# Score matmuls ahead of the key copy, a smaller warm-up tile, a second queue for the last store, and no transfers from GpSimd

## The chip, the cores and the metric

One Trainium2 chip, one of its cores. Five engines work side by side, each through its own list of instructions in order: TensorE (PE, with its weight loads shown as PEld), VectorE (DVE), ScalarE (ACT), GpSimd (POOL) and SyncE (SP), which here only issues transfers. They wait for each other through semaphores. The metric is device microseconds of one execution of the whole program, and times of a kernel are given as the median over its runs.

## The reference

One decoder layer on 1024 prompt tokens and 8 x 8 sample tokens, model width 1024. All is float32. What matters of it:

```python
proj = jnp.einsum('btd,de->bte', x, w_in)
u, gp, q, k, v, gg, fa = jnp.split(proj, SPLIT_IDX, axis=-1)
pool_out, new_buf = pool_mix(u, buf, start_pos, w_map, pool_scale)      # windows 2, 4, 8, 16
log_a = jax.nn.log_sigmoid(fa @ w_a2 + b_a) / GLA_TAU
o, S_new = gla_chunked(q * 64 ** -0.5, k, v, log_a, S)                  # 4 heads, running state S
o = o * lax.rsqrt(jnp.mean(o * o, axis=-1, keepdims=True) + RMS_EPS) * norm_g
mix = jnp.concatenate([pool_out * silu(gp), o * silu(gg)], axis=-1)
h = DEEPNORM_ALPHA * x + mix @ w_out
out = (h - mean(h)) * lax.rsqrt(var(h) + LN_EPS) * ln_g + ln_b
```

The outputs are the layer's `out` for both kinds of tokens, the new pooling buffers and the new states S.

## The kernel before, in words

Tokens lie in nine tiles: eight of 128 prompt tokens (0 to 7) and one of 64 sample tokens (8). For the projections they are grouped in three column chunks of 384, 384 and 320. To keep float32 accuracy each operand is split into a high part (`hi`, rounded to the matmul's format, a ScalarE copy, line 61) and a low part (`lo`, the rest, a VectorE subtraction, line 64), and `mm3` (lines 66 to 70) makes three matmuls of each product: hi x hi, hi x lo, lo x hi. `mm2` does the same for the sample tile.

The order of work is written out by hand; no scheduler moves anything in the part that runs (`manual_schedule`). The stages are:

- **Head.** Input pieces are loaded by SP (the very first by ScalarE), split, and multiplied into the value projection `psv` in eight k-slices. Ahead of that, nine idle matmuls run on a cleared tile `warm` into `psw` (line 189). GpSimd clears `warm` and some other tiles first.
- **Projection groups.** `group(i, c)` computes 128 output columns `i` for the tokens of column chunk `c`, 24 matmuls into `psm`. The order is k, q, u (the pooling input), gp and gg (the gates). At `c == 0` the next weights are split and the ones after that loaded: `load_w` puts a load of 512 KB on SP's queue, into one of two `raw` buffers, so it waits until the buffer's last content was split.
- **Linear attention, interleaved.** `later(delay, fn)` and `tick()` put short pieces between the projection groups; a piece runs at the first tick whose number has reached its due time, and pieces of one tick run in the order of their due times. For chunk c (one token tile) the pieces are `s1a` (turn the keys with two transposes into the bank `pskt`, and copy them to `kt`), `s1b` (four score matmuls per chunk and the mask), `s2p` (keys x values into `psp_`, the state's growth), `s2` (state and masked scores applied, squares, and the state's decay) and `s3` (norm). At one tick they come as: `s1a` of chunk c+1, `s2p` of chunk c, `s1b` of chunk c+1, `s2` of chunk c. The sample tile, chunk 8, has its own times (AT8).
- **Output.** Nine output tiles: `mix @ w_out` into `pso`, then residual, mean and variance, and two VectorE passes with `lng` (the layer norm's gain and bias, broadcast over the partitions). A store `o_y` per tile goes out on SP. The last tile (TAIL) is worked in halves and stored in two pieces, both on SP.

All small PSUM tiles (`pskt`, `psa1`, `psp_`, `pso1`, `psms`, `psmap`) come from one pool of six banks in rotation; `psm` and `psv` have a pool of two. The bank `pskt` holds two things: the turned keys in its first 256 columns and, behind them, the scores of heads 0 and 2 (`pa[0] = pk[:, 256:]`). An access of a bank by one engine waits for the access of another engine to the same bank, whatever the columns. So the scores wait for ScalarE's copy of the turned keys.

GpSimd issues four transfers in the part that runs: `o_sp` (the prompt's final state, line 789, 128 KB), `o_npool` (the pooling buffers, line 485, 270 KB), and the two loads of `lng` (lines 490 and 491, 512 KB each).

The file also holds a second body (`safe`), for inputs whose decay is too strong; it runs only when a flag computed on the way says so, and doesn't run here.

Of the kernel before, what the change touches and what calls it, by code (L numbers as in the profile page):

```python
# [7 lines left out]
F32 = mybir.dt.float32  # L8
FR = mybir.dt.float32r
# [30 lines left out]
class Body:  # L40
# [54 lines left out]
    def emit(self):  # L95
# [82 lines left out]
        rst = ep.tile([128, 384], F32, name="rst")  # L178
        rst2 = ep.tile([128, 320], F32, name="rst2")
        nc.gpsimd.memset(wa2r, 0.0)  # L180
        nc.gpsimd.memset(sel, 0.0)
        nc.gpsimd.memset(eps[:, 0:1], RMS_EPS)
        nc.gpsimd.memset(eps[:, 1:2], LN_EPS)
        nc.scalar.preload_act_table_set(EXP_LN)
        warm = et.tile([128, 512], F32, tag="ab", name="warm")
        nc.gpsimd.memset(warm, 0.0)
        psw = psg.tile([128, 512], F32, tag="g", name="psw")
        for _ in range(9):
            nc.tensor.matmul(psw, warm[:, :128].bitcast(FR), warm.bitcast(FR), start=True, stop=True)  # L189

# [291 lines left out]
        for i in range(4, 16):  # L482
            if i == 14:
                assert not self.due
                nc.gpsimd.dma_start(io["o_npool"], npool)
                for name in ["gl", "pt", "kq"]:
                    self.close(name)
                lnp = self.pool("ln", 1)
                lng = lnp.tile([128, 2, D], F32, name="lng")
                nc.gpsimd.dma_start(lng[:, 0], io["ln_g"].partition_broadcast(128))  # L490
                nc.gpsimd.dma_start(lng[:, 1], io["ln_b"].partition_broadcast(128))
                load_res(0)
                load_res(1)
            for c in range(3):
                group(i, c)
            if i == 14:
                for k in (3, 4, 5):
                    load_wo(k)
# [5 lines left out]
        def out_tile(t):  # L504
# [40 lines left out]
            for cs in parts:  # L545
                nc.vector.scalar_tensor_tensor(hh[:n, cs], hh[:n, cs], mv[:n, 3:4], lng[:n, 1, cs],
                                               op0=ALU.mult, op1=ALU.add)
                nc.sync.dma_start(io["o_y"][t * 128:t * 128 + n, cs], hh[:n, cs])

# [132 lines left out]
    def gla_steps(self, c):  # L682
# [29 lines left out]
        def s1a():  # L712
# [8 lines left out]
            pk = g_tile("pskt")  # L721
            pa = [pk[:, 256:], None]
            for p in range(2):
                nc.tensor.transpose(pk[:n, p * 128:(p + 1) * 128], Kst[:, p], self.ident)
            kt = self.kt8 if sample else gl.tile([128, 256], F32, tag="kt", bufs=1 if self.safe else 2, name="kt")
            nc.scalar.activation(kt[:n], pk[:n, :256], AF.Copy)
            st["kt"], st["pa"] = kt, pa

        def s1b():
            am, pa, Qi = st["am"], st["pa"], st["Qi"]  # L730
            if not self.safe:
                pa[1] = g_tile("psa1")
                for h in range(4):
                    r, p = rows[h % 2], h // 2
                    nc.tensor.matmul(pa[h % 2][:n, p * n:(p + 1) * n], K[r, p], Q[r, p], start=True, stop=True)  # L735
                for e in range(2):
                    nc.vector.tensor_tensor(am[:n, two(e), :n], pa[e][:n, :2 * n].rearrange("s (p t) -> s p t", p=2),
                                            msk[:n, :n].unsqueeze(1).broadcast_to([n, 2, n]), op=ALU.mult)
# [33 lines left out]
        def decay():  # L772
# [15 lines left out]
            if c == 7:  # L788
                nc.gpsimd.dma_start(self.io["o_sp"], sn)

# [70 lines left out]
    def safe_scores(self, c, am, t0, n, sample):  # L861
# [17 lines left out]
        while True:  # L879
# [19 lines left out]
            ml = gl.tile([128, 128], F32, tag="lv", bufs=1, name="lv")  # L899
            nc.gpsimd.dma_start(ml, self.io["lvs" if sample else "lvp"][:, lev])  # L900
            mb = ml[:n, :n].unsqueeze(1).broadcast_to([n, 2, n])
# [23 lines left out]
TAIL = 7  # L925
# [108 lines left out]
```

## Time and profile before

| | us |
|---|---|
| runs shown, median of 3 (lowest, highest) | 398.11 (397.14, 398.34) |
| the profiled execution | 397.98 |
| its span, first to last instruction | 396.2 |
| TensorE busy | 383.3 (97%) |
| VectorE busy | 217.7 (55%) |
| ScalarE busy | 143.6 (36%) |
| GpSimd busy | 8.6 (2%) |
| transfers, mean over the span | 87 GB/s |

The rows shown below come from one profiled execution. A row of the timeline has the start and the duration in microseconds, the engine, the line of the kernel, the operation, the tile written and the tiles read, and in brackets how long the engine had been idle before it and what ended that. A row of the waits has the engine and tile that waited, the work that released it, the sum in microseconds, how many times, and the longest. A row of one line's instructions has the least, the median and the greatest duration in nanoseconds. Queues of issued transfers are named SPq and ACTq.

### The profile page before, as it was taken

How to read it: one execution, taken by the hardware profiler on the slowest of the kernel's cores; microseconds unless marked ns; L12 is line 12 of the kernel's file. 1: busy time of each engine (PE TensorE's matmuls, PEld its weight loads, DVE VectorE, ACT ScalarE, POOL GpSimd, SP SyncE). 2: the span in 40 equal slices, each digit the busy share in tenths (PEclk: the TensorE clock that was granted, in tenths of full speed). 3: DMA queues.
4: the chain of work that ended last, by engine and by line, in shares of the span. 5: the costliest groups of instructions: out<-in, count | busy, mean ns of one | idle time of the engine just before them, and what ended most of it. 6: DMA issues, size and time to landing. Idle time of an engine off the chain costs nothing.

```text
span 396.2 us, 6088 instructions
## 1 busy us (share of the span) xinstructions
PE 383.3 (97%) x2473; PEld 358.3 (90%) x2473; DVE 217.7 (55%) x429; ACT 143.6 (36%) x273; POOL 8.6 (2%) x31
## 2 busy tenths in 40 slices
PE   8999999999999999999999999999999999999991
PEld 7999999999989999999899899999988888888790
DVE  4775555621354778788433321333399565556683
ACT  5554554410023425435766222421283333211200
POOL 1000000000000000000001000100000000000000
PEclk9999999999999999999999999999999999999996
DMA  7960001011100101030103110443330253242321
GB/s 257 393 237 2 19 36 55 3 51 53 55 19 36 53 2 52 3 141 20 55 0 97 53 37 17 161 160 101 132 141 10 96 213 106 108 159 79 103 84 60
DMA packets 11556, 34.29 MB, mean 87 GB/s; under 512 B 1776, under 2 KB 3232, under 8 KB 11264
## 3 DMA queue, kind: packets, MB, share of 16 engines
q1 hardware_dynamic: 10960, 32.24, 23.7%
q0 software_dynamic: 416, 1.46, 1.1%
q8 instruction: 21, 0.34, 0.3%
q10 hardware_dynamic: 144, 0.14, 0.1%
q14 instruction: 15, 0.12, 0.1%
HBM read 27.91 MB, written 5.91 MB: 85 GB/s over the span
## 4 chain that ended last, share of the span: by engine, by line
PE 93%; ACT 3%; issue 1%; DVE 1%; POOL 0%; ACTq 0%; POOLq 0%
PE psm L68 15%; PE psm L69 15%; PE psm L70 15%; PE pso L68 7%; PE pso L69 7%; PE pso L70 7%; PE psv L69 4%; PE psv L68 4%; PE psv L70 4%; PE pskt L735 1%; PE psw L189 1%; PE pso L75 1%; PE pso L78 1%; PE pso L804 1%; PE psms L833 1%
## 5 line engine op out<-in xcount | busy, mean ns | idle before, releaser
L68 PE MATMUL psm<-xc,hl 128*128 128x384 f32 (+1 forms) x384 | 126.2, 329 | 0.0
L70 PE MATMUL psm<-xc,hl 128*128 128x384 f32 (+1 forms) x384 | 125.4, 327 | 0.0
L69 PE MATMUL psm<-xc,hl 128*128 128x384 f32 (+1 forms) x384 | 125.3, 326 | 0.0
L68 PEld LDWEIGHTS psm<-xc,hl 128*128 128x128 f32 x384 | 72.1, 188 | 0.7 <-issue 0.2
L69 PEld LDWEIGHTS psm<-xc,hl 128*128 128x128 f32 x384 | 72.2, 188 | 0.1
L70 PEld LDWEIGHTS psm<-xc,hl 128*128 128x128 f32 x384 | 72.1, 188 | 0.0
L68 PE MATMUL psv<-wv,xc 128*128 128x264 f32 x128 | 36.9, 288 | 0.0
L70 PE MATMUL psv<-wv,xc 128*128 128x264 f32 x128 | 36.7, 287 | 0.0
L69 PE MATMUL psv<-wv,xc 128*128 128x264 f32 x128 | 36.7, 286 | 0.0
L68 PE MATMUL pso<-wo,mx 128*128 128x512 f32 (+1 forms) x85 | 32.0, 377 | 0.0
L70 PE MATMUL pso<-wo,mx 128*128 128x512 f32 (+1 forms) x85 | 32.0, 377 | 0.0
L69 PE MATMUL pso<-wo,mx 128*128 128x512 f32 (+1 forms) x85 | 32.0, 377 | 0.0
L539 ACT ACTIVATE mv<-mv,eps 128x1 f32<-128x1 f32 (+1 forms) x9 | 2.7, 295 | 64.8 <-DVE mv L538 64.8
L403 DVE SCALAR_TENSOR_TENSOR vm<-sg,vecs,vm 128x128 f32<-128x128 f32 (+1 forms) x36 | 10.3, 340 | 27.8 <-ACT sg L397 27.8
L64 DVE TENSOR_TENSOR hl<-raw,hl 128x1024 fp32r<-128x1024 f32 x19 | 23.2, 1223 | 3.8 <-ACT hl L61 3.5
L644 ACT ACTIVATE ue<-psm 128x384 f32<-128x384 f32 (+1 forms) x12 | 5.5, 456 | 53.4 <-PE psm L70 49.5
L68 PEld LDWEIGHTS psv<-wv,xc 128*128 128x128 f32 x128 | 24.6, 192 | 0.1
L69 PEld LDWEIGHTS psv<-wv,xc 128*128 128x128 f32 x128 | 24.5, 191 | 0.1
L532 DVE SCALAR_TENSOR_TENSOR hh<-xr,pso 128x512 f32<-128x512 f32 (+2 forms) x19 | 12.4, 654 | 21.8 <-PE pso L70 21.6
L70 PEld LDWEIGHTS psv<-wv,xc 128*128 128x128 f32 x128 | 24.4, 190 | 0.0
L61 ACT ACTIVATE hl<-raw 128x1024 fp32r<-128x1024 f32 x19 | 19.9, 1051 | 6.4 <-PE psm L70 6.4
L68 PE MATMUL pso<-hl,mx 128*128 128x512 f32 (+1 forms) x51 | 19.3, 379 | 0.0
(236 smaller groups left out, 587.3 us busy)
## 6 DMA issues: line engine op xcount, KB each, us to landing
raw<-wm_dram SPq DMA_DIRECT2D x16, 512.0 KB, 3.5
xr<-x_dram SPq DMA_DIRECT2D x8, 512.0 KB, 4.3
o_y_dram<-hh SPq DMA_DIRECT2D x7, 512.0 KB, 2.9
wr<-w_out_dram SPq DMA_DIRECT2D x5, 512.0 KB, 4.5
s<-s_dram SPq DMA_DIRECT2D x2, 1024.0 KB, 6.7
hl<-xt_dram SPq DMA_DIRECT2D x2, 768.0 KB, 7.0
raw<-w_out_dram SPq DMA_DIRECT2D x3, 512.0 KB, 3.4
hl<-xt_dram SPq DMA_DIRECT2D x2, 640.0 KB, 5.4
```

The lines of the kernel that those rows point to most:

```text
L61: self.nc.scalar.activation(hi.bitcast(FR), raw, AF.Copy)
L64: (on_lo or self.nc.vector).tensor_tensor(lo.bitcast(FR), raw, hi, op=ALU.subtract)
L68: nc.tensor.matmul(ps, ahi.bitcast(FR), bhi.bitcast(FR), start=first, stop=False)
L69: nc.tensor.matmul(ps, ahi.bitcast(FR), blo.bitcast(FR), start=False, stop=False)
L70: nc.tensor.matmul(ps, alo.bitcast(FR), bhi.bitcast(FR), start=False, stop=last)
L75: one = lambda st, sp: nc.tensor.matmul(ps, both.bitcast(FR), bhi.bitcast(FR), start=st, stop=sp)
L78: nc.tensor.matmul(ps[:64], both[:, :64].bitcast(FR), blo.bitcast(FR), start=False, stop=False)
L189: nc.tensor.matmul(psw, warm[:, :128].bitcast(FR), warm.bitcast(FR), start=True, stop=True)
L403: nc.vector.scalar_tensor_tensor(pg, sg[:, to:to + tn], self.norm[:, m:m + 1], pg, op0=ALU.mult, op1=ALU.mult)
L532: nc.vector.scalar_tensor_tensor(hh[:n, s], x[:n, s], ALPHA if n == 128 else 1.0, ps[h][:n, :wd], op0=ALU.mult, op1=ALU.add)
L644: nc.scalar.activation(ue[:, HIST:HIST + np_], src[:, :np_], AF.Copy)
L735: nc.tensor.matmul(pa[h % 2][:n, p * n:(p + 1) * n], K[r, p], Q[r, p], start=True, stop=True)
```

## The change

It has four parts.

1. In `s1a` only the two transposes stay. The copy to `kt` becomes a function `keys()`, called in `s1b` after the four score matmuls and before the masks (in the `safe` body it stays where it was). The bank is the same.
2. `warm` is 128 x 128 in place of 128 x 512, and is cleared first of all on GpSimd; the idle matmuls read it four times over by a broadcast and are as wide as before.
3. The last tile's first half is stored by ScalarE's queue, the second by SP's as before.
4. The four transfers of GpSimd (and the ones of the `safe` body) are issued by SP.

```diff
+        warm = et.tile([128, 128], F32, tag="ab", name="warm")
+        nc.gpsimd.memset(warm, 0.0)
         nc.gpsimd.memset(wa2r, 0.0)
...
-        warm = et.tile([128, 512], F32, tag="ab", name="warm")
-        nc.gpsimd.memset(warm, 0.0)
         psw = psg.tile([128, 512], F32, tag="g", name="psw")
+        wide = warm.bitcast(FR).unsqueeze(1).broadcast_to([128, 4, 128])
         for _ in range(9):
-            nc.tensor.matmul(psw, warm[:, :128].bitcast(FR), warm.bitcast(FR), start=True, stop=True)
+            nc.tensor.matmul(psw.rearrange("p (a c) -> p a c", a=4), warm.bitcast(FR), wide, start=True, stop=True)
...
-                nc.gpsimd.dma_start(io["o_npool"], npool)
+                nc.sync.dma_start(io["o_npool"], npool)
...
-                nc.gpsimd.dma_start(lng[:, 0], io["ln_g"].partition_broadcast(128))
-                nc.gpsimd.dma_start(lng[:, 1], io["ln_b"].partition_broadcast(128))
+                nc.sync.dma_start(lng[:, 0], io["ln_g"].partition_broadcast(128))
+                nc.sync.dma_start(lng[:, 1], io["ln_b"].partition_broadcast(128))
...
-                nc.sync.dma_start(io["o_y"][t * 128:t * 128 + n, cs], hh[:n, cs])
+
+                q = nc.scalar if t == TAIL and cs.start == 0 else nc.sync
+                q.dma_start(io["o_y"][t * 128:t * 128 + n, cs], hh[:n, cs])
...
-            pa = [pk[:, 256:], None]
+            pa = [pk[:, 256:], None, pk]
             for p in range(2):
                 nc.tensor.transpose(pk[:n, p * 128:(p + 1) * 128], Kst[:, p], self.ident)
+            st["pa"] = pa
+            if self.safe:
+                keys()
+
+        def keys():
             kt = self.kt8 if sample else gl.tile([128, 256], F32, tag="kt", bufs=1 if self.safe else 2, name="kt")
-            nc.scalar.activation(kt[:n], pk[:n, :256], AF.Copy)
-            st["kt"], st["pa"] = kt, pa
+            nc.scalar.activation(kt[:n], st["pa"][2][:n, :256], AF.Copy)
+            st["kt"] = kt
...
                     nc.tensor.matmul(pa[h % 2][:n, p * n:(p + 1) * n], K[r, p], Q[r, p], start=True, stop=True)
+
+                keys()
                 for e in range(2):
...
-                nc.gpsimd.dma_start(self.io["o_sp"], sn)
+                nc.sync.dma_start(self.io["o_sp"], sn)
```

On TensorE no instruction moves; what changes is which of them wait. This is its list at the turn from chunk 1 to chunk 2, before (`pskt` and `psa` get the scores, `psp_` the keys x values; the numbers behind names are buffers, and a wait names the engine whose semaphore is waited for):

```order
L724 MATMUL pskt<-ident,K 128x128 [waits PE_49]
L766 MATMUL psp__1462<-vm,kt 64x128 [waits Activation_49]
L735 MATMUL pskt<-Q,K 128x128 [waits Activation_49]
L735 MATMUL psa_1468<-Q,K 128x128
L802 MATMUL psp__1462<-Q,S 128x128
L802 MATMUL pso_1475<-Q,S 128x128
```

And the same place in the changed kernel (its lines 727, 776, 743 and 812):

```order
L727 MATMUL pskt<-ident,K 128x128 [waits PE_49]
L776 MATMUL psp__1460<-vm,kt 64x128 [waits Activation_49]
L743 MATMUL pskt<-Q,K 128x128
L743 MATMUL psa_1466<-Q,K 128x128 [waits Activation_49]
L812 MATMUL psp__1460<-Q,S 128x128
L812 MATMUL pso_1475<-Q,S 128x128 [waits Activation_49]
```

The first score matmul has no wait left. Two waits for ScalarE stand there now that the one for the copy had covered: `psa` takes a bank that ScalarE's `rs` (line 838 before) read last, and `pso` one that `pmix` (line 675 before) read last, both in the group before. On ScalarE the copy keeps its place in the list, but now waits for the scores in place of the transposes, and on VectorE the mask of `pskt` waits for that copy.

SP's list, from the flag's reading to the first loads of the output stage, before:

```order
L200 DMA raw<-wm_dram 128x1024 x5
L697 DMA s_1970<-s_dram 128x2048
L200 DMA raw<-wm_dram 128x1024 x5
L203 DMA raw<-w_out_dram 128x1024
L464 DMA xr<-x_dram 128x1024 x2
L203 DMA raw<-w_out_dram 128x1024
```

And in the changed kernel:

```order
L201 DMA raw<-wm_dram 128x1024 x5
L700 DMA s_1970<-s_dram 128x2048
L201 DMA raw<-wm_dram 128x1024 x2
L799 DMA o_sp_dram<-S 128x256
L201 DMA raw<-wm_dram 128x1024 x3
L204 DMA raw<-w_out_dram 128x1024
L486 DMA o_npool_dram<-npool 128x540
L491 DMA lng<-ln_g_dram 128x1024
L492 DMA lng<-ln_b_dram 128x1024
L465 DMA xr<-x_dram 128x1024 x2
```

`o_sp` stands between two weight loads, and `o_npool` and the two `lng` loads stand ahead of the first residual loads `xr`. At the end of SP's list one of the two stores of the last tile is gone; it stands at the end of ScalarE's list, behind its last `mv`.

More of the change, by code (lines that the diff above doesn't have):

```diff
@@ L899, in safe_scores @@
             ml = gl.tile([128, 128], F32, tag="lv", bufs=1, name="lv")
-            nc.gpsimd.dma_start(ml, self.io["lvs" if sample else "lvp"][:, lev])
+            nc.sync.dma_start(ml, self.io["lvs" if sample else "lvp"][:, lev])
             mb = ml[:n, :n].unsqueeze(1).broadcast_to([n, 2, n])
```

## The prediction

> **What bounds the kernel now.** I read the page first, then the waits of TensorE's two rows (PE for matmuls, PEld for weight loads), then the timeline at the places where the diff cuts.
>
> ```profile
> span 396.2 us, 6088 instructions
> PE 383.3 (97%) x2473; PEld 358.3 (90%) x2473; DVE 217.7 (55%) x429; ACT 143.6 (36%) x273; POOL 8.6 (2%) x31
> PE 93%; ACT 3%; issue 1%; DVE 1%; POOL 0%; ACTq 0%; POOLq 0%
> PE pskt L735 <- ACT kt L726: 1.9, 4, 0.6
> PE psw L189 <- POOL warm L186: 1.7, 1, 1.7
> PEld pskt L735 <- ACT kt L726: 4.5, 9, 0.9
> ```
>
> TensorE is busy 97% of the span and carries 93% of the chain that ended last. The two PE rows are all the waits that the matmul row has: the start (1.7 us) and, inside the kernel, only the score matmuls of line 735, which wait for ScalarE's copy of the turned keys (line 726). The weight-load row lists the same wait in all nine chunks, 4.5 us. No other wait stands in the matmul row. So time taken out of TensorE's queue moves everything behind it, unless a transfer or another engine has less slack than the time gained. The work behind the last matmul is a chain of its own, part 3.
>
> **Part 1, scores no longer wait for the key copy.** Chunk 0, the typical later chunk 1, chunk 7, where ScalarE is late, and chunk 8, the sample tokens:
>
> ```profile
> 111.90 0.18 PEld L735 LDWEIGHTS pskt<-Q,K 64*128 64x128 f32 x1 [0.87 <-ACT kt L726]
> 120.64 0.66 PE L766 MATMUL psp__1333<-vm,kt 128*64 128x128 f32 x8
> 121.49 0.18 PEld L735 LDWEIGHTS pskt<-Q,K 64*128 64x128 f32 x1 [0.44 <-ACT kt L726]
> 193.93 0.51 ACT L675 ACTIVATE pmix<-psmap,vecs 128x320 f32<-128x320 f32 x1
> 195.40 0.66 PE L766 MATMUL psp__2142<-vm,kt 128*64 128x128 f32 x8
> 196.09 0.38 ACT L726 ACTIVATE kt<-pskt 128x256 f32<-128x256 f32 x1
> 196.51 0.18 PEld L735 LDWEIGHTS pskt<-Q,K 64*128 64x128 f32 x1 [0.70 <-ACT kt L726]
> 218.91 0.13 PEld L735 LDWEIGHTS pskt<-Q,K 64*64 64x64 f32 x1 [0.89 <-ACT kt L726]
> ```
>
> What would the gap be without the wait? The program has the same step once without scores between: after the last chunk's L766 the next 64-row weight load follows directly.
>
> ```profile
> 207.50 0.66 PE L766 MATMUL psp__2246<-vm,kt 128*64 128x128 f32 x8
> 208.09 0.18 PEld L802 LDWEIGHTS psp__2246<-Q,S 64*128 64x128 f32 x1 [0.17 <-issue]
> 133.31 0.42 PEld L766 LDWEIGHTS psp__1462<-vm,kt 128*64 128x64 f32 x8 [0.17 <-issue]
> ```
>
> A gap of 0.17 us stays after L766, and also after the transposes (the third row is the load that follows them in a middle chunk). So the gain is 4.5 - 9 x 0.17 = 2.97 us. The distance agrees: L766 to L802 takes 208.09 - 207.50 = 0.59, L766 to the scores took 0.85 in chunk 1 (0.26 to gain) and 1.11 in chunk 7 (0.52). Bounds: 1.9 us if only the idle time of the matmul row returns, 4.5 if no gap stays. I take **2.95**, since the 0.17 is the same step on the same engine.
>
> The copy itself (0.38, nine times) now stands behind the scores on ScalarE, and the masks of line 737 behind the copy, because both read one bank. In chunk 1 the scores would end near 122.0 and the copy near 122.4, about 1 us later than now, when it released the scores at 121.49. What stands behind it on ScalarE is a weight split (1.05 us, used a whole output group later) or the squares, 2.5 us on; its own reader, L766, comes two groups later. The masked scores are read two groups later too. So the late copy costs nothing; without that cover it would give back at most its own 0.38 plus the mask's 0.42 per chunk. What was hidden behind the old wait now shows: `psa1` waits for ScalarE's `rs` and `pso1` for `pmix`, both of the previous group. In chunk 7, the tightest, `pmix` is the later and ends at 193.93 + 0.51 = 194.44; the scores would come at 195.40 + 0.59 = 195.99. Their price is 0.
>
> **Part 2, the warm-up starts earlier.**
>
> ```profile
> 0.73 0.31 POOL L180 MEMSET wa2r<- 128x256 f32 x1 [0.29 <-POOLq L1030]
> 1.08 0.52 POOL L186 MEMSET warm<- 128x512 f32 x1
> 1.66 4.21 PE L189 MATMUL psw<-warm 128*128 128x512 f32 x9 [1.66 <-POOL warm L186]
> 4.39 0.51 ACT L61 ACTIVATE xc<-hl 128x384 fp32r<-128x384 f32 x1
> 5.24 0.33 PEld L68 LDWEIGHTS psv<-wv,xc 128*128 128x128 f32 x1
> 6.77 0.42 PE L70 MATMUL psv<-wv,xc 128*128 128x264 f32 x1
> 6.99 0.33 PE L68 MATMUL psv<-wv,xc 128*128 128x264 f32 x1
> 7.51 0.29 PE L69 MATMUL psv<-wv,xc 128*128 128x264 f32 x1
> 7.63 0.28 PE L70 MATMUL psv<-wv,xc 128*128 128x264 f32 x1
> 9.05 0.96 DVE L64 TENSOR_TENSOR xc<-hl,xc 128x768 fp32r<-128x768 f32 x1 [0.60 <-ACT xc L61]
> 10.80 0.19 PEld L70 LDWEIGHTS psv<-wv,xc 128*128 128x128 f32 x1
> ```
>
> GpSimd's clear of `warm` is now first: it starts at 0.73 and takes about 0.20 (128x512 took 0.52, 128x256 0.31, so 128 columns less are 0.10 less). TensorE followed the old clear by 0.06 (1.60 to 1.66), so it starts near 0.99, 0.67 earlier. The first real weight load does not follow all the way: its data end at 4.39 + 0.51 = 4.90, so it moves from 5.24 to about 4.97, 0.27 earlier. Starts lie 0.22 apart until about 7 us (6.77 to 6.99) and 0.12 apart from then on (7.51 to 7.63): the clock doubles near 7.05, 5.4 after the warm-up began. If it still doubles at 7.05, 0.27 us at the slow pace are worth 0.27 x 0.12/0.22 = 0.15. If it doubles 0.67 earlier as well, those 0.67 us run at full pace and bring another 0.67 x (1 - 0.12/0.22) = 0.30, so 0.45. More than about 0.7 can't be had: the third k-slice's low parts end on VectorE at 9.05 + 0.96 = 10.01, and their first weight load now starts at 10.80. [...] I take **0.3**, between 0.15 and 0.45.
>
> [...]
>
> **Part 3, the tail.**
>
> ```profile
> 386.99 0.28 PE L70 MATMUL pso<-wo,mx 128*128 128x256 f32 x1
> 389.86 1.41 DVE L546 SCALAR_TENSOR_TENSOR hh<-hh,mv,lng 128x512 f32<-128x512 f32 x2
> 388.85 0.20 ACT L540 ACTIVATE mv<-mv 128x1 f32<-128x1 f32 x1
> 391.30 1.25 SPq L548 DMA_DIRECT2D o_y_dram<-hh  x1
> L548 SPq DMA_DIRECT2D o_y_dram<-hh x10: 332/344/1254, 306.0 to 391.3; - x10
> L938 SPq EVENT_SEMAPHORE  x8: 17/17/17, 393.1 to 394.5; - x8
> ```
>
> The last matmul starts at 386.99, 9.2 us before the end. The second half is ready at 389.86 + 1.41 = 391.27 and its store starts at 391.30, so it doesn't stand in line for the first. But its issue takes 1.25 us, against 0.34 for the median store. If that comes from the first store in the same queue, the ScalarE queue takes it away: 1.25 - 0.34 = 0.91. If the DMA engines are what is full, nothing changes. ScalarE is free then (its last work ends at 388.85 + 0.20 = 389.05). I take the middle, **0.45**, with 0 and 0.91 as ends; a loss would need the ScalarE queue to be slower by more than the 0.7 us that the first half is ready earlier.
>
> [...] No row of before tells which it is; without this part the sum would be 3.25 and the time 394.9.
>
> **Part 4, GpSimd's transfers go to SP's queue.** Four issues, each about 0.35 us as the rows of SP's loads below show.
>
> ```profile
> 210.17 0.43 DVE L786 TENSOR_TENSOR S<-S,dec 128x256 f32<-128x256 f32 x1
> 211.25 0.68 POOL L789 DMA_DIRECT2D o_sp_dram<-S  x1 [32.12 <-DVE S L786]
> 221.95 0.33 SPq L200 DMA_DIRECT2D raw<-wm_dram  x1
> 249.20 1.05 ACT L61 ACTIVATE hl<-raw 128x1024 fp32r<-128x1024 f32 x1
> 261.87 0.37 SPq L464 DMA_DIRECT2D xr<-x_dram  x1
> raw<-wm_dram SPq DMA_DIRECT2D x16, 512.0 KB, 3.5
> ```
>
> `o_sp` waits on SP for the state, ready at 210.17 + 0.43 = 210.6, and the weight load behind it leaves at 221.95 anyway. `o_npool` and both `lng` loads go ahead of the `xr` loads at 261.87 and push them by about 1.1 us; both are read with the output tiles, whose first store is at 306.0 by L548's row above. Cost 0, gain 0 (GpSimd is 2% busy).
>
> **Sum.** 2.95 + 0.3 + 0.45 = 3.7. The profiled execution took 397.98 (span 396.2 and 1.78 around it), so 394.3; it lies 0.13 under the median of the runs shown, 398.11, which gives 394.4. I predict **394.4**.
>
> **Rivals.**
> (a) The newly visible waits for `rs` and `pmix` stop TensorE in the middle chunks, and only chunks 0 and 8, which have no such waits, gain: 0.87 + 0.89 - 2 x 0.17 = 1.42. Against it stands the 1.5 us of room in chunk 7. Time 398.11 - 1.42 - 0.75 = 395.9.
> [...]
> (c) TensorE gets ahead and waits elsewhere as long: a weight split or transfer that was just in time. Nearly all is given back, 397.5. Against: no such wait shows in the matmul row, but the trace doesn't tell how much more would make one.
> (d) Slower: SP stands at `o_sp` and holds the weight loads behind it. The load of 221.95 is split on ScalarE at about 249.20 and lands 3.5 after issue (last row); only when SP is held beyond 245 does TensorE wait, and then one for one. To end slower it must be held past about 250, 39 us after the state is ready; at 251, 6 lost less 3.7 won gives 400.4. Nothing in the profile makes it likely.
>
> **Chances.** Forecast 0.76, (a) 0.07, (b) 0.05, (c) 0.08, (d) 0.04. A measurement of this kernel can tell 0.3%, 1.2 us, from no change: the forecast, (a) and (b) are faster, 0.88; (c) the same, 0.08; (d) slower, 0.04. The forecast's own range is 392.9 to 395.6: gains of 1.9 + 0.15 = 2.05 to 4.5 + 0.45 + 0.91 = 5.9; since three terms are hardly at the same end at once, I take 2.5 to 5.2. To 8 in 10 with (a) and (b), and the 1.2 us by which the runs shown differ, it is 392.9 to 396.3.
>
> **What would show it.** L735 without a wait on ACT, and L766 to L735 at 0.59; wrong if PE waits at `psa` or `pso`. The first warm-up matmul near 1.0, the first real weight load near 4.97, and where the spacing falls to 0.12. Two store issues of about 0.35 and a tail from the last matmul shorter than 9.2 us. No issue on GpSimd, and no new PE wait after 221. The prediction is wrong if PE's idle time goes but a wait of the same size appears, or if the time leaves 392.9 to 396.3.

## The result and the profile after

| | before | after |
|---|---|---|
| median of the runs beside each other | 397.73 us (397.14 to 398.34, 6 runs) | 395.26 us (6 runs; five lie between 394.82 and 396.0) |
| ratio, 95% interval | | 0.9939 (0.9923 to 0.9955) |
| the profiled execution, and its span | 397.98, 396.2 us | 394.82, 392.7 us |

The change makes the kernel 2.5 us, 0.6%, faster. The forecast was 394.4, between 392.9 and 396.3. (One of the six runs after was disturbed and took 478 us; it is not in the ratio, and the median of the other five is 395.19.)

The page of the changed kernel:

```profile
span 392.7 us, 6068 instructions
...
PE 96%; DVE 1%; DMA 1%; ACT 0%; issue 0%
```

Its waits of TensorE, first the one row that the matmuls have, then the weight loads' row for the scores:

```profile
PE psw L190 <- POOL warm L181: 1.0, 1, 1.0
...
PEld pskt L743 <- issue: 1.6, 9, 0.2
```

The scores (line 735 before, 743 now) no longer stand in the matmul row, and of the chain, ScalarE's 3% has gone. In the weight-load row 4.5 us became 1.6, with "issue" in place of ScalarE: nine times the gap of 0.17 to 0.18 that stays without any wait. No wait for `psa` or `pso` has come. The same place in chunk 0, by the timeline: the copy now follows the scores, and the mask follows the copy.

```profile
111.04 0.38 ACT L734 ACTIVATE kt<-pskt 128x256 f32<-128x256 f32 x1 [0.41 <-PE psa L743]
111.45 0.42 DVE L747 TENSOR_TENSOR am<-pskt,mask 128x256 f32<-128x256 f32 x1 [4.29 <-ACT kt L734]
```

The head, by the timeline of the changed kernel:

```profile
0.73 0.20 POOL L181 MEMSET warm<- 128x128 f32 x1 [0.29 <-POOLq L1040]
0.99 3.81 PE L190 MATMUL psw<-warm 128*128 128x512 f32 x9 [0.99 <-POOL warm L181]
...
4.89 0.19 PEld L68 LDWEIGHTS psv<-wv,xc 128*128 128x128 f32 x1 [0.52 <-ACT xc L61]
...
5.71 0.28 PE L68 MATMUL psv<-wv,xc 128*128 128x264 f32 x1
...
5.83 0.28 PE L69 MATMUL psv<-wv,xc 128*128 128x264 f32 x1
```

The warm-up starts at 0.99 in place of 1.66, the first real weight load at 4.89 in place of 5.24. The nine idle matmuls take 3.81 us in place of 4.21, so in this execution the full pace begins before they end at 4.80. By 5.71 the starts already lie 0.12 us apart; before, they did so only from 7.15 on. A marker of how far ahead the kernel is after the head is the first matmul into `psfa`, the same step in both. A row of one line's instructions ends with its first and last start. Before, and after:

```profile
L256 PE MATMUL psfa<-ident,fats x9: 271/272/275, 26.8 to 62.7; 128*128 128x128 f32 x8, 64*128 64x64 f32 x1
```

```profile
L257 PE MATMUL psfa<-ident,fats x9: 270/272/274, 25.9 to 61.8; 128*128 128x128 f32 x8, 64*128 64x64 f32 x1
```

So this execution gained 0.9 in the head. The last matmul shows the rest:

```profile
383.11 0.28 PE L70 MATMUL pso<-wo,mx 128*128 128x256 f32 x1
385.97 1.41 DVE L547 SCALAR_TENSOR_TENSOR hh<-hh,mv,lng 128x512 f32<-128x512 f32 x2
386.75 0.36 ACTq L551 DMA_DIRECT2D o_y_dram<-hh  x1
387.40 0.34 SPq L551 DMA_DIRECT2D o_y_dram<-hh  x1
```

It starts 3.88 earlier (386.99 to 383.11): about 0.9 from the head and 2.9 from the scores' wait. But the span fell by only 3.5: the tail behind the last matmul has grown from 9.21 to 9.59. The last VectorE work ends at 385.97 + 1.41 = 387.38, and 5.32 us pass from there to the end; before it was 396.2 - 391.27 = 4.93. Both stores are issued in about 0.35 now, as forecast, and still the end comes later. And 394.82 - 392.7 = 2.1 us lie outside the span, where it was 1.8.

What lies there is the program's exit: each engine leaves the body with a branch that jumps over the `safe` body (line 948, `tc.If`; line 938 before), and then they meet through semaphores. The rows of SP, in the changed kernel and in the kernel before:

```profile
L948 SPq EVENT_SEMAPHORE  x8: 17/17/17, 390.8 to 391.3; - x8
L948 SPq COMPARE_BRANCH  x1: 53/53/53, 387.8 to 387.8; - x1
```

```profile
L938 SPq COMPARE_BRANCH  x1: 53/53/53, 392.6 to 392.6; - x1
```

Before, SP branched at 392.6 and had its first exit semaphore at 393.1 (the row of L938 in the prediction): 0.5 us. Now it branches at 387.8 and the first comes at 390.8: 3.0 us. No part of the prediction had a term for this place.

### The profile page after: what moved, and what is told of

Same layout as the page of the kernel before. It is cut to its first block, busy times and chain, and to the rows that moved or that the text cites. A ratio compares the mean times of both kernels' runs of the same rounds, so it can differ in the third digit from the quotient of the medians.

```text
span 392.7 us, 6068 instructions
## 1 busy us (share of the span) xinstructions
PE 382.2 (97%) x2473; PEld 357.4 (91%) x2473; DVE 217.5 (55%) x429; ACT 144.3 (37%) x273; POOL 6.1 (2%) x27
## 4 chain that ended last, share of the span: by engine, by line
PE 96%; DVE 1%; DMA 1%; ACT 0%; issue 0%
PE psm L68 16%; PE psm L70 16%; PE psm L69 16%; PE pso L68 7%; PE pso L70 7%; PE pso L69 7%; PE psv L70 4%; PE psv L68 4%; PE psv L69 4%; PE pskt L743 1%; PE psms L843 1%; PE pso L75 1%; PE pso L78 1%; PE pso L814 1%; DMA raw<-wv_dram 1%; PE pss L605 1%
## 5 line engine op out<-in xcount | busy, mean ns | idle before, releaser
L404 DVE SCALAR_TENSOR_TENSOR vm<-sg,vecs,vm 128x128 f32<-128x128 f32 (+1 forms) x36 | 10.3, 341 | 27.8 <-ACT sg L398 27.8
L68 PEld LDWEIGHTS psv<-wv,xc 128*128 128x128 f32 x128 | 24.1, 189 | 0.5 <-ACT xc L61 0.5
L70 PEld LDWEIGHTS psv<-wv,xc 128*128 128x128 f32 x128 | 24.1, 188 | 0.3 <-DVE xc L64 0.3
L69 PEld LDWEIGHTS psv<-wv,xc 128*128 128x128 f32 x128 | 24.1, 188 | 0.0
```

The lines of the kernel that those rows point to most:

```text
L68: nc.tensor.matmul(ps, ahi.bitcast(FR), bhi.bitcast(FR), start=first, stop=False)
L69: nc.tensor.matmul(ps, ahi.bitcast(FR), blo.bitcast(FR), start=False, stop=False)
L70: nc.tensor.matmul(ps, alo.bitcast(FR), bhi.bitcast(FR), start=False, stop=last)
L404: nc.vector.scalar_tensor_tensor(pg, sg[:, to:to + tn], self.norm[:, m:m + 1], pg, op0=ALU.mult, op1=ALU.mult)
```

## The experiments

Times are medians; "before" is the kernel before on the same chip in the same session.

| kernel | us (lowest to highest, runs) | before | ratio, 95% interval |
|---|---|---|---|
| part 1 alone | 395.21 (394.95 to 395.4, 5) | 397.94 | 0.9931 (0.9918 to 0.9945) |
| part 2 alone | 397.37 (396.96 to 397.94, 11) | 397.94 | 0.9990 (0.9981 to 0.9999) |
| part 3 alone | 397.87 (396.94 to 398.71, 11) | 397.94 | 0.9996 (0.9987 to 1.0006) |
| part 4 alone | 398.56 (398.2 to 399.62, 11) | 397.94 | 1.0019 (1.0010 to 1.0029) |
| all but part 3 | 396.55 (395.58 to 396.7, 5) | 397.85 | 0.9958 (0.9944 to 0.9972) |
| parts 1 and 2 | 394.54 (393.95 to 395.46, 5) | 397.85 | 0.9918 (0.9903 to 0.9932) |
| part 4, only the four transfers that run | 398.18 (397.44 to 398.67, 11) | 397.85 | 1.0006 (0.9997 to 1.0015) |
| part 4, only those that don't run | 398.88 (398.34 to 399.36, 11) | 397.85 | 1.0028 (1.0019 to 1.0037) |
| whole change, those that don't run kept on GpSimd | 394.27 (394.13 to 394.82, 5) | 397.80 | 0.9915 (0.9900 to 0.9931) |
| before, half of those that don't run on SP | 398.21 (397.79 to 398.92, 12) | 397.80 | 1.0013 (1.0003 to 1.0022) |
| whole change again | 395.31 (394.98 to 395.45, 5) | 397.73 | 0.9937 (0.9923 to 0.9950) |
| those that don't run kept on GpSimd, again | 394.71 (394.33 to 395.87, 5) | 397.73 | 0.9921 (0.9907 to 0.9934) |

### The four parts alone

**Part 1**, the keys' copy behind the scores:

```diff
-            nc.scalar.activation(kt[:n], pk[:n, :256], AF.Copy)
-            st["kt"], st["pa"] = kt, pa
+            st["pa"] = pa
...
                     nc.tensor.matmul(pa[h % 2][:n, p * n:(p + 1) * n], K[r, p], Q[r, p], start=True, stop=True)
+
+                keys()
```

> The kernel before with part 1 alone: the key copy moves behind the score matmuls. The prediction's theory: all nine waits of the score matmuls for the key copy go, the weight loads before the scores keep a gap of about 0.17 us each (1.6 us in all instead of 4.5), nothing takes their place, and the time falls by 2.9 to 3.0 us. The rival that the waits for rs and pmix come in their place expects a wait of PE on psa or pso in the list of waits and a fall of only 1.4 us. The rival that TensorE waits elsewhere as long expects a new wait behind 220 us and a fall under 1 us.

Measured: 397.94 to 395.21, a gain of 2.73 us. The weight loads' wait row of this kernel:

```profile
PEld pskt L740 <- issue: 1.6, 9, 0.2
```

4.5 - 1.6 = 2.9 us came out of TensorE's queue, and nearly all of it reached the end. In this execution `psfa` began at 26.8 as before, so the gain is all part 1's. The copy behind the scores costs nothing that can be seen.

**Part 2**, the small idle tile, cleared first:

```diff
+        warm = et.tile([128, 128], F32, tag="ab", name="warm")
+        nc.gpsimd.memset(warm, 0.0)
         nc.gpsimd.memset(wa2r, 0.0)
...
-        warm = et.tile([128, 512], F32, tag="ab", name="warm")
-        nc.gpsimd.memset(warm, 0.0)
...
-            nc.tensor.matmul(psw, warm[:, :128].bitcast(FR), warm.bitcast(FR), start=True, stop=True)
+            nc.tensor.matmul(psw.rearrange("p (a c) -> p a c", a=4), warm.bitcast(FR), wide, start=True, stop=True)
```

> The kernel before with part 2 alone: warm is 128x128 and cleared first. Theory: the first idle matmul starts near 1.0 instead of 1.66 in every run, but the clock opens at an instant that the program doesn't set, so the gain differs from run to run between 0 and 1 us, and the median falls by 0.3 to 0.6 us. Rival, the clock follows the start of the warm-up: it opens 0.67 earlier than before in every run, and the time falls by 0.45 us with no more spread than before. [...]

Measured: 397.94 to 397.37, a gain of 0.57; the interval of the ratio makes it 0.04 to 0.76. On top of part 1 it was 395.21 to 394.54, 0.67 between two sessions whose kernels before differ by 0.09. It is a small gain and its size is not settled.

**Part 3**, the second queue for the last store:

```diff
-                nc.sync.dma_start(io["o_y"][t * 128:t * 128 + n, cs], hh[:n, cs])
+
+                q = nc.scalar if t == TAIL and cs.start == 0 else nc.sync
+                q.dma_start(io["o_y"][t * 128:t * 128 + n, cs], hh[:n, cs])
```

> The kernel before with part 3 alone: the last tile's first half is stored by ScalarE's queue. The prediction: the issue of the second half takes 0.34 instead of 1.25 us, and the time falls by 0 to 0.9 us. What the profile of the whole change suggests against it: the data land no sooner (about 2.6 us behind the last VectorE work in both), and ScalarE takes its exit branch only behind its store, so the span behind the last VectorE work grows from 4.9 to about 5.3 us: 0 to 0.4 us slower.

Measured: 397.87 against 397.94, no difference (0.9987 to 1.0006). Its tail by the timeline, and the exit rows of SP and ScalarE:

```profile
389.67 1.41 DVE L546 SCALAR_TENSOR_TENSOR hh<-hh,mv,lng 128x512 f32<-128x512 f32 x2
390.44 0.36 ACTq L550 DMA_DIRECT2D o_y_dram<-hh  x1
391.10 0.34 SPq L550 DMA_DIRECT2D o_y_dram<-hh  x1
```

```profile
L940 SPq EVENT_SEMAPHORE  x8: 17/17/17, 392.0 to 394.1; - x8
L940 ACTq COMPARE_BRANCH  x1: 54/54/54, 391.4 to 391.4; - x1
...
L940 ACTq EVENT_SEMAPHORE  x1: 17/17/17, 394.5 to 394.5; - x1
```

The second store's issue took 0.34 us here and 1.25 in the kernel before, the whole 0.91 that the prediction put there. But this length varies by itself where both stores are on SP. The kernel before and part 4 alone begin the first of the two stores at the same instant; the two issues together, before and with part 4 alone:

```profile
390.63 1.92 SPq L548 DMA_DIRECT2D o_y_dram<-hh  x2
```

```profile
390.63 1.01 SPq L548 DMA_DIRECT2D o_y_dram<-hh  x2
```

In the nine profiles with both stores on SP the last issue took 0.33 to 1.25 us, with a median of 0.67; in the five with the second queue it always took 0.34. So part 3 does keep the issue short, and the profile of the kernel before had the longest one.

What the end waits for is the landing of the store, that is, its completion. The profile gives the time from the start of a store's issue to its landing, for all stores `o_y`, before and with part 3 alone (the last store has the longest in both):

```profile
DMA to landing us min/median/max: 2.9/2.9/3.2
```

```profile
DMA to landing us min/median/max: 2.8/2.9/3.0
```

391.30 + 3.2 = 394.5 is where SP's last exit semaphore stands before, and 391.10 + 3.0 = 394.1 where it stands here. That is 3.2 and 394.1 - 391.08 = 3.0 us behind the last VectorE work, hardly earlier: the landing counts from the start of the issue, which VectorE sets, and the length of the issue shows little in it. From SP's last semaphore to the end 1.7 us pass in both (396.2 - 394.5 and 395.8 - 394.1). ScalarE, which now has a store to issue, leaves later (its first exit semaphore comes at 394.5, its jump takes 3.1 us), but no row shows that this costs anything: from the last VectorE work to the end pass 4.72 us, not the 5.3 that I had expected.

**Part 4**, GpSimd's transfers to SP: every `nc.gpsimd.dma_start` becomes `nc.sync.dma_start`, as in the diff of the whole change, and

```diff
             ml = gl.tile([128, 128], F32, tag="lv", bufs=1, name="lv")
-            nc.gpsimd.dma_start(ml, self.io["lvs" if sample else "lvp"][:, lev])
+            nc.sync.dma_start(ml, self.io["lvs" if sample else "lvp"][:, lev])
```

> The kernel before with part 4 alone: o_sp, o_npool and both lng loads are issued by SP. Both theories of the span expect 0: SP stands at o_sp near 211 and the weight load behind it leaves near 222 as before, lng lands long before 300. Theory on the time outside the span: the change's runs lie 2.1 to 2.3 us above their spans, the profiled run of before 1.8. If GpSimd's own transfers are what makes the difference, this kernel shows 2.2 instead of 1.8 and is up to 0.4 us slower; if the last store is what makes it, the run above shows it and this one doesn't.

Measured: 397.94 to 398.56, slower by 0.62, where both theories of the span had 0. The time outside the span is 1.80 us as before, so the theory on that place falls as well. TensorE's matmuls run as before up to the last one, and the last VectorE work ends at 391.27 in both profiles. From there to the end pass 396.8 - 391.27 = 5.53 us in place of 4.93. SP's exit rows of this kernel:

```profile
L938 SPq EVENT_SEMAPHORE  x8: 17/17/17, 394.6 to 395.2; - x8
L938 SPq COMPARE_BRANCH  x1: 53/53/53, 391.7 to 391.7; - x1
```

SP branches earlier than before (391.7, not 392.6) and its first exit semaphore comes later (394.6, not 393.1), 2.9 us behind the branch. Its last store had landed by then (at most 3.1 us after 391.30), and SP's last exit semaphore comes 395.2 - 391.27 = 3.9 us behind the last VectorE work in place of 3.2. No other engine's first exit instruction comes after SP's. The four parts add up to -2.73 - 0.57 - 0.07 + 0.62 = -2.75, and the whole change gave -2.5: there is no large interaction, but there is a loss to explain.

### What makes SP's exit late

Part 4 does two things: it moves four transfers that run, and it moves those of the `safe` body, which SP's exit branch jumps over. SP's list shows how many these are (rows with their counts; in the body that doesn't run, 68 loads `lv` of the levels' masks and four others, 72 together; the expectations below say 76, a miscount of mine). In SP's list the jump goes over 79 instructions before and 151 after part 4; in GpSimd's over 95 and 23. Theory A: the longer jump costs. Theory B: the transfers that run do.

> Part 4 cut in two, first half: only the four transfers that run (o_sp, o_npool, two lng) go to SP; those of the safe body, which does not run, stay on GpSimd. Theory A: the +0.62 of part 4 alone comes from the 76 transfers of the body that is jumped over, which made SP's jump at the end longer; then this kernel ends as before, 397.94 within 0.3, and SP's first exit instruction comes 0.5 us behind its exit branch. Theory B: it comes from the four transfers that run (GpSimd has none left, the exit has 10 in place of 14 instructions on SP); then this kernel is at 398.5 with 2.9 us behind the branch.

Edit (at line 485, and alike at 490, 491 and 789; line 900 stays):

```diff
-                nc.gpsimd.dma_start(io["o_npool"], npool)
+                (nc.gpsimd if self.safe else nc.sync).dma_start(io["o_npool"], npool)
```

> Part 4 cut in two, second half: the four transfers that run stay on GpSimd, the 76 of the safe body, which does not run, are issued by SP. Nothing that is executed changes. Theory A (the longer jump over SP's list): 398.5, and SP's first exit instruction comes about 2.9 us behind its exit branch. Theory B (the four transfers that run): 397.94 within 0.3, and 0.5 us behind the branch.

Edit (the four the other way round, and line 900):

```diff
-                nc.gpsimd.dma_start(io["o_npool"], npool)
+                (nc.sync if self.safe else nc.gpsimd).dma_start(io["o_npool"], npool)
...
-            nc.gpsimd.dma_start(ml, self.io["lvs" if sample else "lvp"][:, lev])
+            nc.sync.dma_start(ml, self.io["lvs" if sample else "lvp"][:, lev])
```

Measured: 398.18 and 398.88 against 397.85. The four transfers that run make no difference that can be told (0.9997 to 1.0015). Those that never run make the kernel 1.03 us slower (1.0019 to 1.0037), though every instruction that is executed is the same. That is more than the 0.6 expected: in the profile the exit accounts for 0.8 (396.6 - 390.90 = 5.70 us behind the last VectorE work in place of 4.93), and the rest is not explained. The exit rows of SP and GpSimd, first with the four that run moved:

```profile
L938 SPq EVENT_SEMAPHORE  x8: 17/17/17, 391.6 to 393.9; - x8
L938 POOLq EVENT_SEMAPHORE  x5: 17/43/43, 181.3 to 181.7; - x5
L938 POOLq COMPARE_BRANCH  x1: 45/45/45, 178.6 to 178.6; - x1
...
L938 SPq COMPARE_BRANCH  x1: 53/53/53, 391.1 to 391.1; - x1
```

and with those that don't run moved:

```profile
L938 SPq EVENT_SEMAPHORE  x8: 17/17/17, 394.5 to 395.0; - x8
L938 POOLq COMPARE_BRANCH  x1: 45/45/45, 251.3 to 251.3; - x1
L938 POOLq EVENT_SEMAPHORE  x1: 17/17/17, 251.8 to 251.8; - x1
...
L938 SPq COMPARE_BRANCH  x1: 53/53/53, 391.6 to 391.6; - x1
```

The two engines mirror each other. Whoever has the 72 transfers behind its branch pays: SP 0.5 us without and 2.9 with them, GpSimd 2.7 with and 0.5 without. GpSimd leaves the body more than 130 us before the end, so its long jump was hidden; SP leaves last, so its own is not. Theory A holds, B falls.

Does the delay grow with the length, or in a step? The kernel before with every second level's load on SP:

```diff
-            nc.gpsimd.dma_start(ml, self.io["lvs" if sample else "lvp"][:, lev])
+            (nc.sync if lev % 2 else nc.gpsimd).dma_start(ml, self.io["lvs" if sample else "lvp"][:, lev])
```

> The kernel before with 34 of the 68 level transfers of the safe body (the odd levels) issued by SP, the other half by GpSimd; nothing that is executed changes. In SP's list the body that is jumped over then has 113 instructions (79 before, 151 with all of them), in GpSimd's 61 (95 before, 23 with none). Delays from the exit branch to the first exit instruction so far: SP 0.5 over 79, 2.9 over 151; GpSimd 2.7 or more over 95, 0.45 over 23. If the jump has a threshold, it lies between 79 and 95: SP 2.9 us and GpSimd 0.45, and the time is 398.5. If the delay grows with the length, SP is near 1.6 and the time within 0.3 of before.

Its exit rows:

```profile
L938 SPq EVENT_SEMAPHORE  x8: 17/17/17, 392.2 to 393.8; - x8
L938 POOLq EVENT_SEMAPHORE  x5: 17/43/5332, 251.8 to 257.5; - x5
L938 POOLq COMPARE_BRANCH  x1: 45/45/45, 251.3 to 251.3; - x1
...
L938 SPq COMPARE_BRANCH  x1: 53/53/53, 391.7 to 391.7; - x1
```

Neither expectation was met. Both engines now jump in 0.5 us, SP over 113 and GpSimd over 61. So for SP nothing happens from 79 to 113, and 2.4 us are added by 151: a step, not a growth; but GpSimd paid 2.7 over 95 already, so the step is not at one count of listed instructions for both. The rows of the two engines have two levels, 0.5 and 2.7 to 3.0 us; what makes the step no row shows, only that the jump is what became longer. The time of this kernel, 398.21, is 0.41 over before with a median span of 396.1 (before 396.0); 2.08 us lie outside the span, where the kernel before has 1.84. More on that below.

### The parts together

**All but part 3** (both last stores on SP):

> Leaves the changed kernel's part 3 out: parts 1, 2 and 4 together, both stores of the last tile on SP's queue. My theory now: the store on ScalarE's queue is worth nothing (alone it gave 397.87 against 397.94), so this kernel takes as long as the whole change, 395.26, within 0.4, and still has SP's late exit (about 3 us from SP's exit branch to its first exit instruction). Rival (the prediction's part 3): the second queue is worth 0.45, so this kernel is at 395.7 or more. Second rival: the whole change has 2.2 us outside the span where all other kernels have 1.8, and the transfer on ScalarE's queue is what adds them together with part 4; then this kernel is at about 394.9 with 1.8 outside.

Measured: 396.55, 1.3 above the whole change, so my theory missed by more than its 0.4, and the second queue seems to be worth something here that it wasn't alone. The tail of this kernel, and SP's exit rows:

```profile
387.14 1.41 DVE L547 SCALAR_TENSOR_TENSOR hh<-hh,mv,lng 128x512 f32<-128x512 f32 x2
387.92 1.59 SPq L549 DMA_DIRECT2D o_y_dram<-hh  x2
```

```profile
L946 SPq EVENT_SEMAPHORE  x8: 17/17/17, 392.5 to 393.0; - x8
...
L946 SPq COMPARE_BRANCH  x1: 53/53/53, 389.6 to 389.6; - x1
```

SP's branch comes 389.6 - 388.55 = 1.05 us behind the last VectorE work, since the issue of the second store took 0.93 us here; in the whole change it is 387.8 - 387.38 = 0.4. Behind either stands the long jump. So the exit takes 394.4 - 388.55 = 5.85 us here and 5.32 there: with SP's long jump on the end's path, the second queue saves 0.5 us in front of it in these two executions. It is no fixed amount: in part 4 alone, with both stores on SP and the long jump, the issue took 0.34 and the exit 5.53. The rest of the difference between the two executions (396.55 and 394.82) lies in the head (`psfa` begins at 27.0 here, at 25.9 in the whole change), which varies from run to run. The two kernels were timed in different sessions and their intervals overlap, so what part 3 is worth beside part 4 is not settled. The second rival falls too: 2.18 us lie outside the span here as well, so it isn't the transfer on ScalarE's queue that puts them there.

**Parts 1 and 2 alone:**

> Parts 1 and 2 alone; stores and GpSimd's transfers as before. My theory: the keys' 2.7 and the warm-up's 0.4 to 0.6 add, and without SP's late exit the time is 394.6 (394.4 to 394.9), below the whole change's 395.26 by 0.6. Rival: the two don't add, because an earlier clock opening also runs ahead of the head's data (the run of part 1 alone had that opening early and gained nothing in the head): 395.2, the same as part 1 alone.

Measured: 394.54, as the theory said, 0.7 under the whole change of another session (the intervals of the ratios just overlap).

**The whole change, with the transfers of the body that doesn't run kept on GpSimd**, and a second time beside the whole change on one chip. Edit against the changed kernel:

```diff
-                nc.sync.dma_start(io["o_npool"], npool)
+                (nc.gpsimd if self.safe else nc.sync).dma_start(io["o_npool"], npool)
...
-            nc.sync.dma_start(ml, self.io["lvs" if sample else "lvp"][:, lev])
+            nc.gpsimd.dma_start(ml, self.io["lvs" if sample else "lvp"][:, lev])
```

> The whole change, but the transfers of the safe body, which does not run, stay on GpSimd; what runs is the changed kernel. By the theory that the loss is SP's jump over the longer body, SP's first exit instruction comes 0.5 us behind its exit branch again, and the time is that of parts 1 and 2 alone, 394.5 (394.2 to 394.9), 0.7 under the whole change's 395.26. Whether the 0.4 us that the whole change spends outside the span is the same effect shows here too: 1.8 outside if it is, 2.2 if not. Rival: the tail of the whole change is short of time for another reason (its two queues, or no transfer on GpSimd); then 395.2 stays.

> The whole change again, beside the next kernel on one chip, so that the two can be compared directly. Theory: 395.3, with about 2.2 us outside the span and SP's first exit instruction 2.9 us behind its exit branch. If the 2.2 outside the span belonged to the session and not to the program, it is 1.8 here and the time 394.9.

> The whole change with the transfers of the body that is jumped over left on GpSimd, a second time. Theory: 394.3 (394.1 to 394.8), 0.6 to 1.0 under the whole change on the same chip: about 0.5 from SP's shorter jump and 0.4 outside the span. Rival: the difference of 1.0 between the earlier two sessions was mostly the clock's opening time, which varies; then the two lie within 0.4 of each other.

Measured: 394.27, and the second time 394.71 beside 395.31 for the whole change. Its tail and SP's exit rows, from the first of the two:

```profile
386.38 1.41 DVE L547 SCALAR_TENSOR_TENSOR hh<-hh,mv,lng 128x512 f32<-128x512 f32 x2
```

```profile
L948 SPq EVENT_SEMAPHORE  x8: 17/17/17, 388.7 to 391.0; - x8
...
L948 SPq COMPARE_BRANCH  x1: 53/53/53, 388.2 to 388.2; - x1
```

The jump takes 0.5 us again, the exit 392.7 - 387.79 = 4.91. The medians over ten runs of each, from two sessions, are 394.5 and 395.3, and their means differ by 0.66 with a standard error of 0.19. In the one session that had both, the difference is 0.6, at the lower edge of what was expected, and one run of the faster kernel (395.87) is slower than all of the other. Medians of the spans there are 392.9 and 393.1; outside the span lie 1.81 and 2.18 us. So of the 0.6, some 0.4 is outside the span, and the shorter jump shows as 0.2 in these medians; the exits of the two profiles there, 394.1 - 389.35 = 4.75 and 393.3 - 387.95 = 5.35, give 0.6. That the whole change has its 2.2 there in both sessions makes it the program's, not the session's. This kernel is 0.85% and 0.79% under the kernel before, against 0.61% and 0.63% for the change as it is. It can't be told from parts 1 and 2 alone (0.82%): part 3 and the four transfers that run bring nothing that shows.

## Why the prediction was right or wrong

**The whole.** 394.4 was forecast, 395.26 measured: faster, inside the range, with 2.5 us of the 3.7 that were summed. Part 1 carries it there; parts 3 and 4 were both off in the same direction, and the range was wide enough for that. Of the terms, part 1 was right, part 2 right as far as it can be told, part 3 absent, and part 4 a loss where the sum had 0: 2.95 + 0.3 + 0.45 + 0 became 2.73 + 0.57 + 0.07 - 0.62 by the parts alone.

**Part 1, right, step by step.** The step "4.5 - 9 x 0.17" gave 2.97; the row became 1.6, so 2.9 left TensorE's queue, and the time fell by 2.73. The weight-load row, not the matmul row with its 1.9, was the one to go by: the matmuls behind a waiting weight load had been held up with it. The copy and the mask came later, and nothing waited for them. The waits for `rs` and `pmix` that would have made rival (a) never showed: the matmuls have no wait on `psa` or `pso`, and no weight load waits there for ScalarE.

**Part 2, the steps right, the size only bounded.** The warm-up starts at 0.99 as forecast, and the first weight load at 4.89 (4.97 forecast). What follows depends on when the full pace begins, and that varies by itself. The prediction called the step in the starts, from 0.22 us apart to 0.12, a doubling of the clock. The rows show the pace alone; the clock that the page of before has as granted is at 0.9 or more in each of its 40 slices but the last, so also in the first 9.9 us:

```profile
PEclk9999999999999999999999999999999999999996
```

Every run has a granted clock, the mean share of the full clock over its span; the profiled execution of before has 0.991. By the row above, the lowest share is that of the last slice, 386.3 to 396.2 us, in which the last matmul starts at 386.99, so this number is no measure of the head's pace. Over 74 runs of that kernel it lies between 0.991 and 0.996; those at 0.991 and 0.992 took 398.05 us in the mean, those at 0.995 and 0.996 397.65. The runs with the early warm-up lie between 0.990 and 0.996. Two executions, where the starts come to lie 0.12 apart, matmuls of the head; first the kernel with only the four running transfers moved, whose warm-up starts at 1.66, then the kernel with all but part 3, whose warm-up starts at 0.99:

```profile
5.32 0.28 PE L68 MATMUL psv<-wv,xc 128*128 128x264 f32 x1
5.45 0.28 PE L69 MATMUL psv<-wv,xc 128*128 128x264 f32 x1
```

```profile
6.98 0.28 PE L70 MATMUL psv<-wv,xc 128*128 128x264 f32 x1
7.10 0.28 PE L68 MATMUL psv<-wv,xc 128*128 128x264 f32 x1
```

The late warm-up runs at full pace from 5.32 on, the early one only from about 6.9. So the full pace doesn't follow the warm-up's start, as the prediction's 0.45 end assumed. Nor does the program alone set it: of the whole change there are two profiles, and its starts lie 0.12 apart from 5.71 on in the one (the head above) and from 6.76 on in the other. What sets it no row shows. With the low end of 0.15 for this part the forecast would have been 394.6, nearer to 395.26, but by chance: for this part alone 0.57 was measured. Over 14 profiles the first `psfa` began at 26.0 to 26.8 (mean 26.6) with the late warm-up and at 25.9 to 27.8 (mean 26.5) with the early one: the profiles don't show the gain, the medians of the times put it at about 0.6 with an interval from 0.04. The 0.9 that the profile of the changed kernel shows in the head is more luck than part 2. The chances and the range of the forecast also count with a rival (b), in which a break between the warm-up and the data delays the full pace; no run shows such a delay. With parts 1 and 2 alone TensorE stood idle there for 0.26 us, and the starts lie 0.12 apart from 5.85 on (the row below). In the kernel with all but part 3, where the full pace begins only at about 6.9, the real matmuls follow the warm-up without a gap at 5.00. So of these two executions the one with the break has the earlier full pace.

```profile
5.03 0.39 PE L68 MATMUL psv<-wv,xc 128*128 128x264 f32 x1 [0.26 <-ACT xc L61]
```

**Part 3, wrong.** The step that failed is "I take the middle": that an issue of 1.25 us shortened to 0.34 ends the kernel earlier by half the difference. The issue was shorter by the full 0.91 in the profile, and the time wasn't (397.87 against 397.94). What stands in front of the end is not the length of the issue but the landing of the store, which comes 2.7 to 3.4 us after the issue starts in the kernels with a short jump. And the 1.25 was one execution's value: with both stores on SP it varies from 0.33 to 1.25. Only where SP's long jump stands behind the issue did part of it count, 0.5 us in the pair of executions above.

**Part 4, wrong.** The step that failed is "Four issues ... Cost 0, gain 0". For the four that run it is right (398.18 against 397.85, no difference that can be told). But the diff also moves 72 transfers of a body that never runs, and I gave them no line in the sum, because nothing of them is executed. They lengthened the jump at the end of the engine that leaves last: 2.4 us at the branch, and about 0.6 of it at the end, since SP would have waited for its last store anyway. From the last VectorE work to the end, the nine profiles with SP's short jump take 4.7 to 5.4 us (mean 5.0) and the five with the long one 5.3 to 5.9 (mean 5.55); by the times it was 0.62 and 1.03. The forecast that would show it, "a tail from the last matmul shorter than 9.2 us", came out as 9.59 and pointed at the place. Rival (d), the slower one, looked for the loss on SP at `o_sp`; it was on SP, but at the exit.

**Rival (c)** did not happen: no new wait of the matmuls has come in the changed kernel (its weight loads wait 0.8 us for data, in the head), and the loss at the exit is there without any gain to give back, in part 4 alone.

## What to carry to other kernels

Code that is jumped over wasn't free here (part 4, with 72 transfers that never run, cost 0.62 us, and those 72 alone 1.03): it belongs in the sum as an entry of its own, by engine, and what it can cost is read from the gap between an engine's exit branch and its first exit instruction. Give the bulk of a body that rarely runs to an engine that leaves early, as GpSimd does here, more than 130 us before the end, and keep the list of the engine that leaves last short. In a wait row of weight loads the whole sum counted, less the gap that an unhindered load of the same kind keeps: 4.5 - 1.6 = 2.9 us here, of which 2.73 arrived at the end. And before shortening the issue of a last store, look at what ends behind it: here the end waited for the store's landing, about 3 us after the start of its issue, and a shorter issue hardly brought that forward.

## What the runs showed of the hardware that I had not expected

- **Jumps cost 0.5 us or about 3, with nothing between in these runs.** SP 0.5 over 79 and 113 instructions, 2.9 to 3.0 over 151; GpSimd 0.5 over 23 and 61, 2.7 over 95 (with its `lng` loads issued just before, 6.6 us pass from its branch to its first exit semaphore in the kernel before, 251.6 to 258.2). In the rows of ScalarE above it is 3.1 in the kernel with part 3 alone.
- **The time outside the span belongs to the program.** It is 1.6 to 1.9 us in every run of nine kernels, and 2.0 to 2.3 in every run of the whole change (both sessions), of all but part 3, and of the half-and-half kernel, which executes the same instructions as the kernel before. It costs these about 0.3 to 0.4 us and is in no row of a trace. Keeping the 72 transfers on GpSimd took it out of the whole change (1.77 and 1.81), but it doesn't go with SP's jump: part 4 alone has the long jump and 1.80 outside. What it is stays open.
- **The full pace begins at its own time.** Between executions of the head it begins somewhere from before 4.8 us to about 7.1 us, and that doesn't go with the start of the warm-up. The first `psfa` moves by up to 1.9 us, from 25.9 to 27.8; in the execution where it comes last, the second of the kernel that keeps those that don't run on GpSimd, the head's weight loads waited 1.2 us for ScalarE's `xc` and 0.7 for VectorE's. A head's gain is therefore not to be read from a single profile.
